# Two gate projections of the second half by seven-product blocks, and another place for the weight-sum jobs

## The chip, the cores and the metric

One core of one Trainium2 chip runs the whole program. The metric is device microseconds of one execution, median of three runs: 1961.64 us (1959.43 to 1966.48) for the kernel before. The engines are TensorE (PE, its weight loads PEld), VectorE (DVE), ScalarE (ACT), GpSimd (POOL) and SyncE (SP), which here only issues transfers. Each engine executes its own queue in order.

## The reference, cut to what matters

One layer: a recurrent branch (RG-LRU), a gated linear attention branch (GLA), each projected to the model width, multiplied by a sigmoid gate and added; then a SwiGLU FFN. The model width is 1024, the FFN 2816, the prompt 1024 tokens, and 8 sequences of 4 sample tokens are beside it.

```python
h = _rmsnorm(x, norm1_g) * (1.0 + sc1) + sh1
u = h @ w_in
u_x, u_g, u_q, u_k, u_v, u_r, u_lr, u_ga, u_gb = jnp.split(u, idx, axis=-1)
xc, new_conv = _causal_conv(u_x, conv_buf, conv_w, conv_b)
h_lru, h_T = _rg_lru(xc, h0, lru_wa, lru_ba, lru_wx, lru_bx, lru_lambda)
y_a = h_lru * jax.nn.gelu(u_g)
...
y_b = o.reshape(B, T, GLA_DV_TOTAL) * jax.nn.silu(u_r)
m = jax.nn.sigmoid(u_ga) * (y_a @ proj_a) + jax.nn.sigmoid(u_gb) * (y_b @ proj_b)
x = (x + gt1 * (m @ w_out)).astype(x.dtype)
h2 = _rmsnorm(x, norm2_g) * (1.0 + sc2) + sh2
f1, f2 = jnp.split(h2 @ ffn_w1, 2, axis=-1)
x = (x + gt2 * ((jax.nn.silu(f1) * f2) @ ffn_w2)).astype(x.dtype)
```

## The kernel before, in words

The tokens are worked in two halves, one after the other: half A (`hf == 0`) has 512 prompt tokens, half B (`hf == 1`) the other 512 and the 32 sample tokens, so 544 columns in two pieces of 272. Features lie on the partitions, in tiles of 128. Every float32 product is made as three matmuls of a rounded high part and a low part of weight and input: `gemm` (L439) issues for each of 8 input tiles and each piece high by high, high by low and low by high. Weights come raw by SP into five `raw` buffers (`load_raw`, L143); `split_w` (L151) makes the high part on ScalarE (L154) and the low part on VectorE (L155) in one of three `hl` buffers, placed by priority some 70 instructions ahead.

`branches` (L1652) runs a half: the attention, with the recurrence `lru` (L1145) as filler; then `y_b_tiles` (L1046), which splits the eight `yb`; then `merge_b`, `merge_a` (or in B `merge_a_fast`), and `back` (output projection, second norm, FFN). `merge_b` (L1182) makes for each of 8 output tiles j the gate product `gbps` (w_in tile T_GB + j, L1189) and the branch product `pbps` (proj_b, L1204), and stores gate times branch in `mb`, a tile of the pool X (8 slots). Half A makes each gate one step ahead. At each yield the rest of the recurrence goes on by two steps: `lru_x` (conv input, `uxps`), `lru_gate` (L1088: `g1`, `g2`, the decay `la` and its partner `hh`), `lru_g` (L1112: `ugps`, the scan, `ya`). The large tiles `ya`, `yb`, `la` and others share the pool S of 17 slots; in half B alone block 9 has its `la` and `lh` in X. T is a pool of six slots.

`merge_a` (half A) makes for each j the gate `gaps` and the branch product `paps` (proj_a, two loads of five tiles, `pa0` and `pa1`). `merge_a_fast` (half B) makes branch products 0 to 3 first and holds them, then couples of two gates by seven products of half the size (`gates_fast`, L1226; `products`, L1410), with sums of input blocks (`block_sums`, L1378) and sums of weight blocks. Couples of the FFN's first product (`ffn1_fast`, L1516; tiles `fa`, `fb`, `fc`, weights `fw`) are made in the same way. Their TensorE order is as written (`as_written`); all else is ordered by a scheduler, by priority and by readiness in a model of time.

The weight sums are made on the fly in half A's and half B's first stages and kept in DRAM. `weight_sums` (L348, `sums_of`): two loads of 512 KB by SP into `raw`, four VectorE operations (L352 to L355), two stores by POOL. `paced_sums` (L362, `sums_late`): 20 jobs of two steps. The first step has for each of two buffers `sums` (there are two in all) a one-column copy on POOL from the tile `pace[0]`, which makes the load wait for that tile, and a load by POOL's queue; the second has four VectorE operations (L392 to L396), the first put behind all VectorE work written before, and two stores by POOL (L398). Jobs 0 to 3 are for FFN couples, 4 to 7 and the last 4 for the second FFN product (384 columns a piece), those between for the gates (256 columns).

```python
            for v in range(2):
                pool.tensor_copy(r[v][:, 0:1], pace[0][:, 0:1])
                pool.dma_start(rv[v], src[v])
            yield 1
```

## Time and profile before

| | us |
|---|---|
| median of the runs | 1961.64 |
| the profiled execution, its own time | 1964.05 |
| its span in the profile | 1962.3 |
| TensorE busy | 1928.1 (98%) |
| VectorE busy | 1361.2 (69%) |
| ScalarE busy | 972.8 (50%) |
| GpSimd busy | 148.8 (8%) |
| mean granted clock | 0.994 |

The profile is of one execution. Busy times are sums over a whole span in which stages have different limits; TensorE's matmuls overlap, so the distance between their starts, not their duration, is what one costs. Along the span half A's merge lies at about 300 to 560 us, its couples 11 to 21 at about 790 to 905, half B's merge at about 1278 to 1533. A wait is named by the instruction that waits and the one that released it.

### The profile page before, as it was taken

Reading aid. Unit: us, or ns where it says so; the run is one execution under the profiler, and the core shown is the slowest. Engines: PE = TensorE matmul, PEld = TensorE weight load, DVE = VectorE, ACT = ScalarE, POOL = GpSimd, SP = SyncE. Lnnn points to the kernel's source line nnn. Section 1 sums busy time; section 2 is a strip of 40 time slices with the busy share of each in tenths; the row PEclk is TensorE's granted clock in tenths of the full one; section 3 lists DMA queues with packets and bytes.
Section 4 is the critical chain, followed back from the end, with each engine's and each line's share of the span. In section 5 each row is a group of like instructions: output and inputs, shape, how many; then the busy total and the mean of one; then the engine's idle time right before and its main releaser. Section 6 shows DMA issues by size and latency. Waiting matters only on the chain. (4 is left out here: it accounts for less than half of the span.)

```text
span 1962.3 us, 33970 instructions
## 1 busy us (share of the span) xinstructions
PE 1928.1 (98%) x13380; PEld 1756.9 (90%) x13380; DVE 1361.2 (69%) x2420; ACT 972.8 (50%) x1559; POOL 148.8 (8%) x279
## 2 busy tenths in 40 slices
PE   9999999998999999999999999999999999999997
PEld 5877777786899998999899998999999999999997
DVE  5648587666658774677674497786467688888867
ACT  4536376533235552555353365665245354666653
POOL 0000001122100000000000001141201000000000
PEclk9999999998999999999999999999999999999999
DMA  8344325476764456554332412334446634555553
GB/s 341 116 154 175 117 92 197 153 262 250 267 227 156 129 179 234 196 185 156 118 119 68 145 50 88 127 121 141 146 140 228 202 130 130 176 169 180 176 164 105
DMA packets 122241, 319.24 MB, mean 163 GB/s; under 512 B 14561, under 2 KB 29665, under 8 KB 122081
## 3 DMA queue, kind: packets, MB, share of 16 engines
q1 hardware_dynamic: 107536, 263.89, 41.5%
q0 software_dynamic: 14000, 52.62, 7.4%
q8 instruction: 105, 1.72, 0.4%
q10 hardware_dynamic: 544, 0.56, 0.1%
q14 instruction: 56, 0.45, 0.1%
HBM read 278.42 MB, written 38.59 MB: 162 GB/s over the span
## 5 line engine op out<-in xcount | busy, mean ns | idle before, releaser
L155 DVE TENSOR_TENSOR fwa_hl<-fwa,fwa_hl 128x1024 fp32r<-128x1024 f32 (+1 forms) x57 | 68.8, 1207 | 44.4 <-ACT fwa_hl L154 43.8
L155 DVE TENSOR_TENSOR fwb_hl<-fwb,fwb_hl 128x1024 fp32r<-128x1024 f32 (+1 forms) x64 | 77.2, 1207 | 27.4 <-ACT fwb_hl L154 27.1
L154 ACT ACTIVATE fwa_hl<-fwa 128x1024 fp32r<-128x1024 f32 (+1 forms) x57 | 59.3, 1040 | 43.7 <-PE fapsa L1431 10.7
L154 ACT ACTIVATE fwb_hl<-fwb 128x1024 fp32r<-128x1024 f32 (+1 forms) x64 | 66.6, 1041 | 23.4 <-PE fcpsb L1431 9.0
L454 PE MATMUL f3psa<-faa,f3a_hl 128*128 128x512 f32 x176 | 68.7, 391 | 1.2 <-DVE f3a_hl L155 1.2
L452 PE MATMUL f3psa<-faa,f3a_hl 128*128 128x512 f32 x176 | 68.7, 390 | 0.6 <-ACT f3a_hl L154 0.6
L453 PE MATMUL f3psa<-faa,f3a_hl 128*128 128x512 f32 x176 | 68.6, 390 | 0.0
L154 ACT ACTIVATE f3a_hl<-f3a_raw 128x768 fp32r<-128x768 f32 (+1 forms) x32 | 25.3, 792 | 56.7 <-PE f3psa L454 37.8
L352 DVE TENSOR_TENSOR s_raw<-s_raw 128x512 f32<-128x512 f32 x16 | 11.1, 692 | 49.3 <-DMA s_raw<-in_ffn 49.3
L454 PEld LDWEIGHTS f3psa<-faa,f3a_hl 128*128 128x128 f32 x176 | 33.0, 188 | 8.9 <-DVE f3a_hl L155 2.1
L452 PEld LDWEIGHTS f3psa<-faa,f3a_hl 128*128 128x128 f32 x176 | 33.0, 188 | 7.7 <-ACT f3a_hl L154 1.0
L453 PEld LDWEIGHTS f3psa<-faa,f3a_hl 128*128 128x128 f32 x176 | 33.1, 188 | 6.8
L155 DVE TENSOR_TENSOR f3a_hl<-f3a_raw,f3a_hl 128x768 fp32r<-128x768 f32 (+1 forms) x32 | 28.3, 888 | 14.3 <-ACT f3a_hl L154 14.3
L454 PE MATMUL wopsb<-mb,wob_hl 128*128 128x272 f32 x128 | 36.9, 288 | 0.0
L452 PE MATMUL wopsb<-mb,wob_hl 128*128 128x272 f32 x128 | 36.9, 289 | 0.0
L453 PE MATMUL wopsb<-mb,wob_hl 128*128 128x272 f32 x128 | 36.8, 288 | 0.0
L453 PE MATMUL wopsa<-ma,woa_hl 128*128 128x256 f32 x128 | 36.4, 284 | 0.0
L454 PE MATMUL wopsa<-ma,woa_hl 128*128 128x256 f32 x128 | 36.2, 283 | 0.0
L452 PE MATMUL wopsa<-ma,woa_hl 128*128 128x256 f32 x128 | 36.1, 283 | 0.0
L1616 POOL DMA_DIRECT2D out_yb<-yb x4 | 2.9, 720 | 407.6 <-DVE yb L1613 406.9
L452 PE MATMUL uxpsa<-h1a,uxpsa_hl 128*128 128x512 f32 x80 | 32.3, 403 | 0.0
L155 DVE TENSOR_TENSOR fvb_hl<-fvb,fvb_hl 128x768 fp32r<-128x768 f32 x28 | 26.8, 956 | 7.7 <-ACT fvb_hl L154 7.3
(2402 smaller groups left out, 7986.7 us busy)
## 6 DMA issues: line engine op xcount, KB each, us to landing
ada<-in_ada_w SPq DMA_DIRECT2D x48, 512.0 KB, 5.5
fwb<-wsum SPq DMA_DIRECT2D x72, 256.0 KB, 3.6
s_raw<-in_ffn SPq DMA_DIRECT2D x32, 512.0 KB, 4.8
wsum<-s_raw POOLq DMA_DIRECT2D x32, 512.0 KB, 3.8
fwa<-wsum SPq DMA_DIRECT2D x64, 256.0 KB, 3.4
fwb<-in_ffn SPq DMA_DIRECT2D x54, 256.0 KB, 3.7
fwa<-in_ffn SPq DMA_DIRECT2D x48, 256.0 KB, 3.2
woa_raw<-in_w_out SPq DMA_DIRECT2D x13, 512.0 KB, 3.6
```

The source lines that it names most:

```text
L154: act.activation(hl[:, 0, :n], raw[:, :n], AF.Copy)
L155: dve.tensor_sub(hl[:, 1, :n], raw[:, :n], hl[:, 0, :n].bitcast(F32))
L352: dve.tensor_add(r2[:, 512:1024], r2[:, 0:512], r2[:, 512:1024])
L452: pe.matmul(out, wh, x[:, o:o + w], start=st, stop=False)
L453: pe.matmul(out, wh, x[:, N + o:N + o + w], start=False, stop=False)
L454: pe.matmul(out, wl, x[:, o:o + w], start=False, stop=en)
L1616: (queues[j // 2 % len(queues)]).dma_start(out[:, j:j + 2, o:o + w], y2)
```

## The change

Half B makes its gates T_GB by couples as well. Its `merge_b` becomes `branch_b`: the eight products with proj_b are made first and copied to `mb`, with three steps of the recurrence at each yield. `merge_fast` makes block sums and four held products (two of them now in `sums` buffers instead of T), then four couples for T_GB (`k`), each followed by the multiplication onto `mb`, and four for T_GA (`h`) as before. The sums of the new couples' weights are eight more jobs, 28 in all. Their places change: in A's `merge_b` at j = 3 to 6 (before 4 to 7), in A's `merge_a` both steps at j = 1 to 5 (before one step at each j), eleven beside A's couples f = 11 to 21 (none before), in half B one at each product of `branch_b` (as many before, beside gate and branch product), none in `merge_fast` (before four). `sums_of` steps in `merge_b` are at j = 0 to 6 (before 1 to 7). In half A too, `la` and `lh` of block 9 are in X. The columns of the w_in tiles from T_GB on are stored in the order KORD.

```diff
--- before.py
+++ after.py
@@ -82,7 +82,7 @@
     axp = ctx.enter_context(tc.tile_pool(name="axp", bufs=2, space=PSUM))
     drp = ctx.enter_context(tc.tile_pool(name="drp", bufs=1, space=bass.MemoryType.DRAM))
     wsum = {f: drp.tile([P, 2048], F32, name=f"wsum{f}") for f in range(FAST[1], NF)}
-    wsumg = [drp.tile([P, 2048], F32, name=f"wsumg{c}") for c in range(GATES)]
+    wsumg = {(t, c): drp.tile([P, 2048], F32, name=f"wsumg{t}_{c}") for t in (T_GB, T_GA) for c in range(GATES)}
     wsum2 = {(q, g): drp.tile([P, 1536], F32, name=f"wsumf{q}{g}") for q in range(4) for g in range(2)}
 
     def S(name, dt=F32):
@@ -377,8 +377,9 @@
         for f in range(FAST[1], FAST[0]):
             columns(wsum[f], [I["ffn1"][2 * f + v] for v in range(2)])
         rows(0)
-        for c in range(GATES):
-            columns(wsumg[c], [I["w_in"][T_GA + 2 * c + v] for v in range(2)])
+        for t in (T_GB, T_GA):
+            for c in range(GATES):
+                columns(wsumg[t, c], [I["w_in"][t + 2 * c + v] for v in range(2)])
         rows(1)
         for k, (u, src, to) in enumerate(jobs):
             r = [wp.tile([P, 768], F32, tag="sums", name=f"sums{k}{v}", bufs=2) for v in range(2)]
...
@@ -1097,7 +1098,7 @@
                 for o, p in s.over(t, g):
                     act.activation(o, p, AF.Tanh, scale=0.5, bias=vh[:, b:b + 1])
             dve.scalar_tensor_tensor(ti[:, :N], ti[:, :N], 1.0, xc[:, :N], op0=OP.add, op1=OP.mult)
-            if s.hf == 0 or nb < NR - 1:
+            if nb < NR - 1:
                 both = S("la" + n)
                 a, hh = both[:, :N], both[:, 544:544 + N]
             else:
@@ -1191,13 +1192,15 @@
                 for t, p in s.over(tg, ps):
                     act.activation(t, p, AF.Tanh, scale=0.5)
 
-            lag = 1 - s.hf
-            if lag:
-                first(0)
+            first(0)
             for j in range(KD):
                 n = f"{s.n}{j}"
-                if j + lag < KD:
-                    first(j + lag)
+                if j + 1 < KD:
+                    first(j + 1)
+                if 3 <= j < 7:
+                    pace[0] = tgs[j]
+                    next(sums_late, None)
+                if j + 1 < KD:
                     yield 5.2
                 tg = tgs.pop(j)
                 p2 = s.wide("pbps" + n)
@@ -1206,12 +1209,27 @@
                 for (t, p), (o, _) in zip(s.over(tg, p2), s.over(m, p2)):
                     dve.scalar_tensor_tensor(o, t, 1.0, p, op0=OP.add, op1=OP.mult)
                 s.mb.append(m)
-                pace[0] = tg
-                if s.hf == 0 and j:
+                if 3 <= j < 7:
+                    next(sums_late, None)
+                if j < 7:
                     next(sums_of, None)
-                if s.hf or j >= 4:
-                    next(sums_late, None)
-                    next(sums_late, None)
+                yield 5.2
+
+        def branch_b(s):
+
+            s.mb = []
+            pace[0] = s.y_b[0][:, :2].bitcast(F32)
+            for j in range(KD):
+                n = f"{s.n}{j}"
+                next(sums_late, None)
+                ps = s.wide("pbps" + n)
+                s.gemm(ps, load_w(I["proj_b"][j], 1024, "pb" + n), 8, s.y_b)
+                m = xp.tile([P, 544], F32, tag="X", name="mb" + n)
+                for o, p in s.over(m, ps):
+                    act.activation(o, p, AF.Copy)
+                s.mb.append(m)
+                pace[0] = m
+                next(sums_late, None)
                 yield 5.2
 
         def gate_a(s, j):
@@ -1223,12 +1241,12 @@
             pace[0] = tg
             return tg
 
-        def gates_fast(s, c, product):
+        def gates_fast(s, b, c, product):
 
             N, W = s.N, s.N // 2
             hi, lo = slice(0, W), slice(W, N)
-            pa, pb, pc = [mm(f"h{k}ps{s.n}{c}")[:, 0, :W] for k in "abc"]
-            v1, v2 = T(f"gc{s.n}{c}"), T(f"gd{s.n}{c}")
+            pa, pb, pc = [mm(f"{b}{k}ps{s.n}{c}")[:, 0, :W] for k in "abc"]
+            v1, v2 = T(f"{b}c{s.n}{c}"), T(f"{b}d{s.n}{c}")
             product(pa, "11", True)
             s.snap(v1[:, lo], pa)
             product(pb, "t1", True)
@@ -1272,34 +1290,40 @@
             s.m = []
             for j in range(KD):
                 tg = s.gate_a(j)
+                if 1 <= j < 6:
+                    next(sums_late, None)
                 s.join(j, tg, s.over(tg, s.branch_a(j)))
                 s.keep_m(j)
-                next(sums_late, None)
+                if 1 <= j < 6:
+                    next(sums_late, None)
                 if j % 3 < 2 and j < 7:
                     next(sums_of, None)
 
-        def merge_a_fast(s):
+        def merge_fast(s):
 
             s.m = []
             N, b, held = s.N, s.block_sums(s.h, "h"), []
             two = S("pa" + s.n)
             for j in range(4):
-                t = two[:, j * N:(j + 1) * N] if j < 2 else T(f"pa{s.n}{j}")[:, :N]
+                next(b, None)
+                t = two[:, j * N:(j + 1) * N] if j < 2 else wp.tile([P, 768], F32, tag="sums", name=f"pa{s.n}{j}", bufs=2)[:, :N]
                 for o, p in s.over(t, s.branch_a(j)):
                     act.activation(o, p, AF.Copy)
                 held.append(t)
-                next(b, None)
             drain(b)
             units = []
-            for c in range(GATES):
-                w1, w2, sm = I["w_in"][T_GA + 2 * c], I["w_in"][T_GA + 2 * c + 1], wsumg[c]
-                units += [w1[:, 0:512], sm[:, 1536:2048], sm[:, 0:512], sm[:, 512:1024], sm[:, 1024:1536], w1[:, 512:1024],
-                          w2[:, 512:1024]]
+            for g in (T_GB, T_GA):
+                for c in range(GATES):
+                    w1, w2, sm = I["w_in"][g + 2 * c], I["w_in"][g + 2 * c + 1], wsumg[g, c]
+                    units += [w1[:, 0:512], sm[:, 1536:2048], sm[:, 0:512], sm[:, 512:1024], sm[:, 1024:1536], w1[:, 512:1024],
+                              w2[:, 512:1024]]
             begin = len(traced())
             product = s.products(units, 512, s.bs, "gw" + s.n)
             for c in range(GATES):
-                tgs = s.gates_fast(c, product)
-                next(sums_late, None)
+                for m, t in zip(s.mb[2 * c:], s.gates_fast("k", c, product)):
+                    dve.scalar_tensor_tensor(m[:, :N], t[:, :N], 1.0, m[:, :N], op0=OP.add, op1=OP.mult)
+            for c in range(GATES):
+                tgs = s.gates_fast("h", c, product)
                 if c == GATES - 1:
                     s.keep_m(*range(2 * c))
                 for i in range(2):
@@ -1307,8 +1331,6 @@
                     s.join(j, tg, [(tg[:, :N], held[j])] if j < 4 else s.over(tg, s.branch_a(j)))
                     if c == GATES - 1:
                         s.keep_m(j)
-                    if j >= 4:
-                        next(sums_late, None)
             drain(sums_late)
             as_written(begin, (mybir.EngineType.PE,))
 
@@ -1536,6 +1558,8 @@
                 product(pa, "t2", False)
                 s.snap(v1[:, hi], pa)
                 product(pb, "22", False)
+                if s.hf == 0 and f >= 11:
+                    next(sums_late, None)
                 yield 6
                 product(pa, "t3", False)
                 s.snap(v2[:, hi], pa)
@@ -1552,6 +1576,10 @@
                     s.late = tg
                 else:
                     s.keep(f, tg)
+                if s.hf == 0:
+                    if f >= 11:
+                        next(sums_late, None)
+                    pace[0] = tg
                 yield 4.5
             as_written(begin, (mybir.EngineType.PE,))
 
@@ -1667,15 +1695,17 @@
             mix(chain(iter([6]), s.head_norm(1)), fill)
             drain(r)
             s.y_b_tiles()
-            for w in s.merge_b():
+            for w in s.branch_b() if s.hf else s.merge_b():
                 next(l, None)
                 next(l, None)
+                if s.hf:
+                    next(l, None)
                 s.ada(1)
             drain(l)
             drain(s.adas)
             if s.hf:
                 pool.dma_start(O["tails"], tails)
-            s.merge_a_fast() if s.hf else s.merge_a()
+            s.merge_fast() if s.hf else s.merge_a()
             s.back()
 
     A, B = Half(0), Half(1)
...
```

## Rows read from the trace of the kernel before

**Rows 1.** The page, part 1: busy us (share of the span) and instructions

```profile
PE 1928.1 (98%) x13380; PEld 1756.9 (90%) x13380; DVE 1361.2 (69%) x2420; ACT 972.8 (50%) x1559; POOL 148.8 (8%) x279
```

**Rows 2.** TensorE's waits, whole span: us in total, times, longest

```profile
PE papsa L454 <- DVE pa1a_hl L155: 7.5, 1, 7.5
...
PE hbpsb L1429 <- ACT t12hb L1403: 0.9, 1, 0.9
```

**Rows 3.** Stretches: us, PE PEld DVE ACT POOL busy (instructions), clock, DMA share, GB/s

```profile
460.00:480.00 20.00, 12.52 (x43) 9.58 (x42) 14.85 (x25) 7.56 (x10) 10.48 (x10) 0.74 0.57 199
...
480.00:500.00 20.00, 20.00 (x90) 16.57 (x89) 11.94 (x17) 5.95 (x8) 2.42 (x5) 1.00 0.79 274
...
785.00:905.00 120.00, 120.00 (x967) 118.38 (x966) 83.96 (x120) 67.38 (x108) 2.13 (x4) 1.00 0.60 194
...
1380.00:1400.00 20.00, 20.00 (x163) 20.00 (x162) 8.34 (x16) 4.30 (x7) 4.67 (x8) 1.00 0.47 159
```

**Rows 4.** Order of time, VectorE: start, us, line, out<-in, count [idle before]

```profile
453.10 0.69 DVE L352 TENSOR_TENSOR s_raw<-s_raw 128x512 f32<-128x512 f32 x1 [5.74 <-DMA s_raw<-in_ffn]
...
463.75 0.43 DVE L392 TENSOR_TENSOR sums<-sums 128x256 f32<-128x256 f32 x1 [3.95 <-DMA sums<-in_ffn]
...
468.87 0.82 DVE L155 TENSOR_TENSOR pa1a_hl<-pa1a_raw,pa1a_hl 128x640 fp32r<-128x640 f32 x1
```

**Rows 5.** Order of time, ScalarE, block 9 of half A

```profile
416.10 0.68 ACT L1098 ACTIVATE tia<-g2a,vh 128x512 f32<-128x512 f32 x1
...
448.12 0.80 ACT L1106 ACTIVATE laa<-tra,sp 128x512 f32<-128x512 f32 x1
```

**Rows 6.** Order of time, TensorE: two products, two block products

```profile
1381.80 0.29 PE L452 MATMUL gbpsb4l<-h1b,gbpsb_hl 128*128 128x272 f32 x1
...
1387.77 0.29 PE L452 MATMUL pbpsb4l<-ybb,pbb_hl 128*128 128x272 f32 x1
...
1476.24 0.29 PE L1429 MATMUL hbpsb<-h1b,gwb_hl 128*128 128x272 f32 x1
...
1477.75 0.29 PE L1429 MATMUL hapsb<-t3hb,gwb_hl 128*128 128x272 f32 x1
```

**Rows 7.** Order of time, TensorE, couples of half A's FFN

```profile
839.83 0.28 PE L1429 MATMUL fcpsa<-h2a,fwa_hl 128*128 128x256 f32 x1
...
847.02 0.28 PE L1429 MATMUL fbpsa<-h2a,fwa_hl 128*128 128x256 f32 x1
...
849.89 0.28 PE L1429 MATMUL fcpsa<-h2a,fwa_hl 128*128 128x256 f32 x1
```

**Rows 8.** Order of time, VectorE and GpSimd, a job of half B

```profile
1394.86 0.42 DVE L392 TENSOR_TENSOR sums<-sums 128x256 f32<-128x256 f32 x1 [0.48 <-DMA sums<-in_w_in]
...
1397.98 0.73 POOL L398 DMA_DIRECT2D wsumg<-sums  x1 [0.93 <-DVE sums L396]
...
1400.94 0.19 POOL L387 COPY sums<-gbb 128x1 f32<-128x1 f32 x1 [0.75 <-DMA wsumg<-sums]
1401.18 1.43 POOL L388 DMA_DIRECT2D sums<-in_w_in  x2
```

**Rows 9.** Transfers in 1275:1435, then 300:460: KB each, median us to landing

```profile
sums<-in_w_in POOLq DMA_DIRECT2D x16, 256.0 KB, 3.3
...
sums<-in_ffn POOLq DMA_DIRECT2D x8, 256.0 KB, 4.9
...
wsum<-sums POOLq DMA_DIRECT2D x6, 256.0 KB, 5.6
```

**Rows 10.** Order of time, VectorE, a split in half A's FFN couples

```profile
842.60 1.23 DVE L155 TENSOR_TENSOR fwa_hl<-fwa,fwa_hl 128x1024 fp32r<-128x1024 f32 x1 [0.72 <-ACT fwa_hl L154]
```

**Rows 11.** Order of time, TensorE and VectorE, start of half B's merge

```profile
1277.56 0.29 PE L452 MATMUL gbpsb0l<-h1b,gbpsb_hl 128*128 128x272 f32 x1
...
1288.97 5.17 DVE L189 TENSOR_TENSOR ybb<-srb,ybb 128x544 fp32r<-128x544 f32 x8
```

**Rows 12.** Instructions on the tile sums: duration ns min/median/max, starts

```profile
L387 POOL COPY sums<-gbb x16: 179/185/1076, 1285.1 to 1424.1; 128x1 f32<-128x1 f32 x16
```

More of the change, by code (lines that the diff above doesn't have):

```diff
@@ L665, in proj_h @@
             ps = s.wide(name)
-            s.gemm(ps, w_in_tile(t, name), KD, s.h, split=split, order=KORD if T_GA <= t < T_GB else None)
+            s.gemm(ps, w_in_tile(t, name), KD, s.h, split=split, order=KORD if t >= T_GA else None)
             return ps
@@ L1753, in _pack @@
     wi = _tiles(np.concatenate([w[:, :o[6]], w[:, o[7]:]], 1))
-    wg = wi[T_GA:T_GB].reshape(T_GB - T_GA, P, KD, P)[:, :, list(KORD)]
-    wi[T_GA:T_GB] = wg.reshape(T_GB - T_GA, P, D)
+    wg = wi[T_GA:].reshape(len(wi) - T_GA, P, KD, P)[:, :, list(KORD)]
+    wi[T_GA:] = wg.reshape(len(wi) - T_GA, P, D)
     a["w_in"] = wi
```

## The prediction

> **What bounds the kernel now.** Begin with the shares of the engines on the page: TensorE is busy 1928.1 us, 98% of the span [rows 1]. Nothing but TensorE work, or one of its few stalls, can shorten this kernel, and any other engine matters only where it makes TensorE wait. So the second view is the list of TensorE's waits. One is large: `papsa` in line 454 waits 7.5 us, once, for VectorE's split of `pa1a_hl` [rows 2]. The third view, the stretches, shows what that stall costs in all: 460 to 480 us issued 43 matmuls of 512 columns where the next 20 us issued 90, and its granted clock averaged 0.74, so part of it at the lower of the two levels, 1.2 and 2.4 GHz, where the next stretch has 1.00 [rows 3]. 47 matmuls at 20/90 = 0.222 us are 10.4 us: 7.5 of waiting and about 2.9 in which the matmuls after it ran at the low level. The fourth view, the order of time on VectorE and ScalarE, says why. VectorE executes its queue in order, and stood 5.74 us for a load of `s_raw` (a sum job of `weight_sums`) and 3.95 us for the load of a paced sum job (L392), both queued ahead of the split that TensorE needed [rows 4]. ScalarE had the last recurrent block's gate input at 416.10, but its decay `laa` came at 448.12 [rows 5]: that tile takes a slot of the pool S (17 slots), which then holds eight `ya`, eight `yb` and one older `la`; the slot came free when the last product with `yb` began. The recurrence's tail (L1122 to L189) then ran in front of the split too.
>
> **The change, part by part.** Sums are made against the profiled execution, 1964.05 us (span 1962.3 and 1.75 around it), which is 2.4 above the median of the three runs, 1961.64; the forecast is moved down by that 2.4.
>
> (a) *First half, its last block and its jobs.* `la9` and `lh9` now come from pool X also in half A. X has 8 slots; the branch products hold at most six until block 9 ends, so the wait for S goes and the chain of block 9 starts some 30 us earlier. Jobs run at j = 3..6 in place of 4..7, none at the last product nor at the first `merge_a` step, and the `sums_of` jobs are one step earlier (0..6). Nothing on VectorE then waits for a transfer just before `pa1a_hl`. Gain: 10.4 us at most, 0 at least; I take all, because both causes in [rows 4, 5] are removed.
>
> (b) *Second half, first gates by blocks.* Removed: 8 products of 48 matmuls; one lasts 1387.77 - 1381.80 = 5.97 us, 47.8 us together. Added: 4 couples of 7 block products; one is 1477.75 - 1476.24 = 1.51 us, a couple 10.57, four 42.3 [rows 6]. Gain 5.5 us. Weight splits grow from 2048 to 3584 columns a couple on ScalarE and VectorE; the existing gate couples carry this load without a stall, so it costs nothing there.
>
> (c) *Block sums* of h start one product earlier, and two of the held products lie in the `sums` slots, not in T (six slots, of which the block sums take four at a time). The stall of `hbpsb` at the first couple, 0.9 us [rows 2], should go: gain 0.9, at least 0.
>
> (d) *Jobs beside A's couples 11 to 21.* The 8 new jobs, and those moved, make 11 jobs here, one in each couple. A couple lasts 849.89 - 839.83 = 10.06 us [rows 7]. VectorE is busy 84.0 of 120 us [rows 3], 7.0 a couple; four additions at 0.42 [rows 8] make 8.7: it fits. What may not fit is the job's own loop, since both `sums` buffers belong to one job: additions, stores by POOL, landing, pacing copies, loads, landing. From one job of half B [rows 8]: first addition 1394.86 to second store 1397.98 is 3.1 us; the next copy, released by that store's landing, is at 1400.94, 3.0 later; the two loads begin at 1401.18 and take 1.43, so the second begins 1.0 after the copy; it lands 3.3 later (the median in that stretch [rows 9]). Loop: 10.4 us. With the landings of the first half's stretch, 5.6 for the store and 4.9 for the load [rows 9], it is 14.6. The DMA share of the couples is 0.60 [rows 3], already above the 0.47 of half B's stretch, before the jobs add 1 MB a couple (256 KB four times), but they have no bursts of 512 KB loads, as that first stretch has; so I stay near the lower end: load 3.9, store 3.0, loop 11.0. When the loop is longer than the couple, L392 blocks VectorE, with the splits behind it and TensorE behind those. Cover: a split ends at 843.83 and its first matmul is at 847.02, 3.2 us [rows 7, 10]. Ten intervals of 0.94 less 3.2: **cost 6 us**; ends 0 (10.4 gives 3.4 of lag, all but covered) and 42 (14.6).
>
> Beside this stands a price that only a page gives: the Trainium skill, DMA: Bandwidth & Descriptors, section on the anatomy of one DMA on the GpSimd path, fits such a transfer with 2.0 us plus bytes over 436 GB/s, an estimate of 2.6 us for 256 KB. By it the loop is 9.3 us, below the couple, and (d) costs nothing; the landings of [rows 9], 3.3 to 5.6, are all longer, so the trace doesn't bear it out here.
>
> (e) *`merge_a` of A:* five jobs in steps 1 to 5, one a step, where before one took two steps. A step is 24 + 30 matmuls, 12.0 us at 0.222. With the landings of that half the loop is 14.6, so lag grows by 2.6 in four intervals, 10.4; one split tile of 15 matmuls covers 3.3. Ends 0 and 7; I take 3.5.
>
> (f) *Start of `branch_b`:* its first product needs all `yb`, where the removed gate product stood between. That one began at 1277.56, and the eight splits of `yb` lasted from 1288.97 to 1294.14, 0.65 us each [rows 11]. In place of the gate product `ux7` and `ug5`, which followed it, can run from 1277.56, at 5.97 each until 1289.5; by then the first `yb` is there, and the others come faster than the product eats them (0.75 us a tile). I take 0; if the product is queued ahead of `ug5`, 6.
>
> (g) *End of `branch_b`:* products 5 to 7 have no recurrent work between, 5.97 us each, with a job of 10.4 each: VectorE waits some 4 and then 9 us. What queues behind L392 are the splits for `proj_a` and the block sums; two split tiles are ahead. I take 2; ends 0 and 6.
>
> Other edits (names, order of w_in columns, the pace variable) cost nothing: matmul count and bytes are the same. The jobs that left `merge_fast` hid no wait, so that is nothing either.
>
> Sum: -10.4 - 5.5 - 0.9 + 6 + 3.5 + 0 + 2 = -5.3; 1964.05 - 5.3 - 2.4 = **1956 us**.
>
> **The rivals.**
> *R1, the loops keep pace.* (d), (e) and (g) cost 0 to 6 together, because landings are near 3 us: -16.8 to -10.8, so 1945 to 1951. For it: in half B at a cadence of 11.9 us L392 waited only 0.48 us [rows 8]. Against: the couples are shorter and the DMA share higher.
> *R2, slower: the pacing copies are late.* In each job POOL's two copies stand between landing and load. They take 0.18 us as a rule and 1.08 at the worst [rows 12]; on a VectorE busy nine tenths both may be near the worst, 1.8 us more, so the loop is 12.8, and (d) costs 10 times 2.7 less 3.2, 24 us. With (e) at 7 and (g) at 6 the sum is +20: 1982. It decides against the change as soon as the loop of (d) is above 11.5 us, where it costs 11.3 and (e) and (g) at 5.5 eat the rest. The rule behind such lateness is in the Trainium skill, SBUF — State Buffer, section Who interferes with whom: a VectorE instruction with two SBUF inputs keeps out a GpSimd instruction that reads SBUF until it ends; of the 16 copies in [rows 12] the median is at the minimum, so the trace bears it out for few.
> *R3, the change doesn't do what it says in A:* the stall at `papsa` stays or moves by a step, since jobs are denser there: -6.4 + 11.5 = +5, 1967.
>
> **How the numbers follow.** Forecast (costs of 6 to 20 together) 0.42, R1 0.33, R2 0.16, R3 0.09. A measurement of this kernel can tell about 0.5%, 9.8 us, from no change. Faster by more (below 1951.8): R1 and a little of the forecast, 0.36. Slower by more (above 1971.4): R2 and a little of R3, 0.17. Within: 0.47. Range: 1944 (all gains, no cost) to 1975 (R2 with half of its price beyond the forecast).
>
> **What would show it.** (a) No wait of `papsa` above 2 us near 470, clock 1.00, and `laa` of block 9 within 5 us of its tanh. (b) 336 matmuls of the k-couples where 384 of `gbpsb` were. (c) No wait of `hbpsb`. (d) The distance of `fcpsa` between couples: 10.06 if the loop keeps pace, 11 if it binds, with `sums` L392 waiting for DMA each time. (e), (g) L392's waits in 490 to 560 and near the last `pbpsb`. The prediction is wrong if A's couples keep 10.06 us (faster), or if they take above 12 (slower).

## The result, and the profile after

The change makes the kernel slower. The kernel after takes 2025.62 us (2022.01 to 2032.46), the kernel before 1964.02 in the same runs, a ratio of 1.0322 (95% interval 1.0307 to 1.0338); the forecast was 1956 us with a range up to 1975. The page of after, its span, the engines and the first addition of the paced jobs (L393, L392 before):

```profile
span 2026.2 us, 34080 instructions
PE 1940.8 (96%) x13332; PEld 1763.9 (87%) x13332; DVE 1381.1 (68%) x2462; ACT 990.2 (49%) x1593; POOL 185.0 (9%) x327
...
L393 DVE TENSOR_TENSOR sums<-sums 128x256 f32<-128x256 f32 (+1 forms) x28 | 12.9, 461 | 89.2 <-DMA sums<-in_w_in 68.5
```

TensorE has 12.7 us more busy time than in [rows 1] for 48 matmuls fewer, so a part ran at the lower level of its clock, and idles some 51 us more. The last row is the lead: the 28 first additions found VectorE idle for 89.2 us, waiting for the jobs' loads; the 20 of the kernel before waited 4.5 us. TensorE's waits, in half A's merges, in couples 11 to 21 with the start of half B, and from half B's u_x products on (us in total, times, longest):

```profile
PE gapsa L455 <- DVE gapsa_hl L155: 6.4, 4, 4.1
...
PE fapsa L1453 <- DVE fwa_hl L155: 7.8, 4, 2.2
PE nps1b L460 <- DVE acc1b L488: 7.7, 1, 7.7
PE fapsa L1451 <- ACT vaa L1459: 4.2, 7, 0.9
PE fbpsa L1453 <- DVE fwa_hl L155: 4.1, 3, 3.0
...
PE pbpsb0l L453 <- ACT ybb L188: 7.4, 1, 7.4
PE papsb1l L455 <- DVE pa0b_hl L155: 6.5, 1, 6.5
PE pbpsb1l L453 <- ACT trb L1099: 6.5, 1, 6.5
PE pbpsb3l L453 <- ACT trb L1099: 2.0, 1, 2.0
```

[rows 2] show two waits, `papsa` 7.5 and `hbpsb` 0.9. Both are gone, and these nine, with others of 2.3 us and less, stand in their place. The stretches (us, then busy time of PE, PEld, DVE, ACT and POOL, PE clock, DMA share, GB/s):

```profile
790.00:902.00 112.00, 97.73 (x767) 95.03 (x766) 71.45 (x119) 53.28 (x84) 27.36 (x42) 0.97 0.68 212
902.00:955.00 53.00, 38.95 (x239) 33.77 (x238) 32.91 (x56) 21.63 (x36) 14.29 (x24) 0.94 0.64 202
1280.00:1360.00 80.00, 63.62 (x433) 59.34 (x432) 55.51 (x111) 42.05 (x74) 18.30 (x28) 0.85 0.35 111
1444.00:1484.00 40.00, 33.19 (x243) 32.53 (x242) 23.86 (x43) 13.53 (x27) 6.41 (x8) 0.87 0.51 158
1484.00:1526.00 42.00, 42.00 (x338) 42.00 (x337) 25.80 (x32) 24.29 (x42) 0.00 (x0) 1.00 0.56 173
```

[rows 3] had 785 to 905 without a gap at clock 1.00. Only the last of these five, the k couples, is like that now. The first start of a tile's matmuls in each trace (for the couples the last start of `fapsa`) gives the account by stretch; before and after are differences of two such starts, the last column is the growth:

| stretch | before | after | change |
|---|---|---|---|
| start to half A's output product (`wopsa` 562.0, 559.4) | 562.0 | 559.4 | -2.6 |
| from there to the end of the couples (last `fapsa` 902.9, 926.2) | 340.9 | 366.8 | +25.9 |
| to half B's norm and u_x products (`uxpsb0l` 1155.4, 1192.3) | 252.5 | 266.1 | +13.6 |
| to the first held product (`papsb0l` 1429.6, 1443.6), 47.8 us of gate products gone | 274.2 | 251.3 | +24.9 beside those 47.8 |
| four held products (to 1459.5, 1483.5) | 29.9 | 39.9 | +10.0 |
| k couples (to 1525.6) | 0 | 42.1 | 5.7 less than the 47.8 |
| h couples and the rest (`wopsb` 1533.1, 1597.5) | 73.6 | 71.9 | -1.7 |

Together +64.4; the spans differ by 63.9. The k couples bring what (b) said; the loss is elsewhere, where the jobs stand. The first additions beside the couples, in order of time on VectorE, with what each waited:

```profile
819.08 0.42 DVE L393 TENSOR_TENSOR sums<-sums 128x256 f32<-128x256 f32 x1 [2.68 <-DMA sums<-in_w_in]
831.86 0.42 DVE L393 TENSOR_TENSOR sums<-sums 128x256 f32<-128x256 f32 x1 [4.95 <-DMA sums<-in_w_in]
845.20 0.43 DVE L393 TENSOR_TENSOR sums<-sums 128x256 f32<-128x256 f32 x1 [4.11 <-DMA sums<-in_w_in]
858.31 0.42 DVE L393 TENSOR_TENSOR sums<-sums 128x256 f32<-128x256 f32 x1 [5.16 <-DMA sums<-in_w_in]
874.05 0.42 DVE L393 TENSOR_TENSOR sums<-sums 128x256 f32<-128x256 f32 x1 [6.53 <-DMA sums<-in_w_in]
...
938.30 0.42 DVE L393 TENSOR_TENSOR sums<-sums 128x256 f32<-128x256 f32 x1 [5.18 <-DMA sums<-in_w_in]
```

From 804.82 to 938.30 eleven additions follow each other at 13.35 us on average, where a couple has 10.06 [rows 7]. One round, on POOL:

```profile
833.04 0.71 POOL L399 DMA_DIRECT2D wsumg<-sums  x1 [4.97 <-DVE sums L395]
834.97 0.73 POOL L399 DMA_DIRECT2D wsumg<-sums  x1 [1.22 <-DVE sums L397]
835.70 0.82 POOL L388 COPY sums<-fta 128x1 f32<-128x1 f32 x1
836.82 0.71 POOL L389 DMA_DIRECT2D sums<-in_w_in  x1 [0.30 <-POOL sums L388]
839.22 0.18 POOL L388 COPY sums<-fta 128x1 f32<-128x1 f32 x1 [1.69 <-DMA wsumg<-sums]
839.70 0.73 POOL L389 DMA_DIRECT2D sums<-in_w_in  x1 [0.30 <-POOL sums L388]
```

From the first addition (831.86) to the second store (834.97) 3.1 us as in [rows 8]; to the copy that this store's landing released (839.22) 4.25, not 3.0; to the next first addition (845.20), which the load issued at 839.70 released, 6.0. That is the loop named in (d); POOL is busy for 3.9 us of it and waits for the rest.

### The profile page after: what moved, and what is told of

Read it like the earlier page. It is cut to its first block, busy times and chain, and to the rows that moved or that the text cites. A ratio compares the mean times of both kernels' runs of the same rounds, so it can differ in the third digit from the quotient of the medians.

```text
span 2026.2 us, 34080 instructions
## 1 busy us (share of the span) xinstructions
PE 1940.8 (96%) x13332; PEld 1763.9 (87%) x13332; DVE 1381.1 (68%) x2462; ACT 990.2 (49%) x1593; POOL 185.0 (9%) x327
## 5 line engine op out<-in xcount | busy, mean ns | idle before, releaser
L393 DVE TENSOR_TENSOR sums<-sums 128x256 f32<-128x256 f32 (+1 forms) x28 | 12.9, 461 | 89.2 <-DMA sums<-in_w_in 68.5
L455 PE MATMUL f3psa<-faa,f3a_hl 128*128 128x512 f32 x176 | 69.7, 397 | 3.5 <-DVE f3a_hl L155 3.4
L155 DVE TENSOR_TENSOR gwb_hl<-gwb,gwb_hl 128x1024 fp32r<-128x1024 f32 x28 | 34.3, 1225 | 27.1 <-ACT gwb_hl L154 23.4
L352 DVE TENSOR_TENSOR s_raw<-s_raw 128x512 f32<-128x512 f32 x16 | 11.1, 691 | 46.4 <-DMA s_raw<-in_ffn 46.4
```

The costliest lines, as they stand in the source:

```text
L155: dve.tensor_sub(hl[:, 1, :n], raw[:, :n], hl[:, 0, :n].bitcast(F32))
L352: dve.tensor_add(r2[:, 512:1024], r2[:, 0:512], r2[:, 512:1024])
L393: dve.tensor_add(r2[:, 1], r2[:, 0], r2[:, 1])
L455: pe.matmul(out, wl, x[:, o:o + w], start=False, stop=en)
```

## The experiments

Theory L: the jobs' loop through their two buffers is longer than the work beside it, and since the addition stands in VectorE's queue ahead of splits, the whole kernel goes at the loop's pace. Rivals: D1, the jobs' traffic makes weights late; D2, VectorE has too much arithmetic; and for half B, Q (the order of TensorE's queue) and V (VectorE is late there without any job). Where gate couples read sums of other weights instead of a job left out, size and traffic stay. A time without a range is that of one execution; the kernel before took from 1957.4 to 1967.2 us in its own, so small differences are read from the stretches of the traces, not from the totals.

**Couples without jobs (e1).**

```diff
-                if s.hf == 0 and f >= 11:
-                    next(sums_late, None)
...
-                    if f >= 11:
-                        next(sums_late, None)
...
+            if 9 <= k < 20:
+                continue
```

> The eleven sum jobs beside couples 11 to 21 of half A are left out (additions, loads, copies and stores); the gate couples that would read their sums read other sums of the same size, so the output differs. The kernel after takes 2025.6 us; there couples 11 to 21 end 25.9 us late against before and half B's norm another 13.7. Theory L (loop): the jobs' own round through their two buffers takes 13.4 us where a couple has 10.06 us of matmuls, and its first addition, standing in VectorE's queue, stops the couple's splits; the jobs' copies and stores on POOL's queue also delay half B's load of x. L expects the last couple product near 903 us (926 with the jobs), half B's norm product near 920 (953), and 1986 us in all (1982 to 1992). Theory D (traffic or VectorE's load, not the loop) expects the same here, and is told apart by the next runs. Theory E (the couples are late for what stands ahead of them, la9 and lh9 or the denser jobs of the merges) expects the couples to stay over 915 and the time over 2010.

Measured: 1980.8 us, before 1957.4 beside it. From half A's output product to the last couple product 339.6 us (after 366.8, before 340.9), from there to the norm product of half B 16.0 (27.0, 16.1). Between 790 and 930 TensorE has no wait. So the jobs cost the couples 27 us and half B's start 11; theory E is out. The time is 1 us below the expected 1982 to 1992, and still 23.4 over before: the rest lies in half B, whose stretch from the first u_x product to `wopsb` is 20.0 us longer than before.

**No additions (e2).**

```diff
-            dve.tensor_add(r2[:, 1], r2[:, 0], r2[:, 1])
+            if not 9 <= k < 20:
+                dve.tensor_add(r2[:, 1], r2[:, 0], r2[:, 1])
+                ...
```

> Beside couples 11 to 21 of half A the jobs keep their copies, loads and stores, and only their four additions on VectorE are left out (the sums stored there are the raw halves, so the output differs). Theory L (a VectorE that stands at the jobs' additions): the couples run at 10 us again, the last product near 903 to 906 us; half B's x load still stands behind copies and stores on POOL's queue, so part of the 13.7 us at half B's start stays: 1988 to 2002 us. Theory D1 (the traffic of the jobs makes the couples' weights late): the couples stay some 20 us late and the time over 2015. Theory D2 (VectorE's arithmetic): like L.

Measured: 2000.35 us. The couples take 342.9, 3.3 over e1: not 27. With all transfers and no additions, the stretch 820 to 902 was full, at a higher DMA share than in the kernel after:

```profile
820.00:902.00 82.00, 82.00 (x678) 81.59 (x677) 59.84 (x89) 47.71 (x78) 27.16 (x44) 1.00 0.83 262
PE f3psa L454 <- ACT f3a_hl L154: 6.2, 1, 6.2
PE nps1b L461 <- DVE acc1b L489: 4.9, 1, 4.9
...
912.24 2.16 POOL L543 DMA_DIRECT2D xb<-in_xb  x4
917.38 0.66 ACT L487 ACTIVATE sq1b<-xb 128x544 f32<-128x544 f32 x1 [12.69 <-DMA xb<-in_xb]
```

The same stretch of after has PE busy 67.7 us, a DMA share of 0.67 and 212 GB/s. So 262 GB/s don't hold TensorE up, and D1 falls. Half B's start stays late (28.6 us): its four loads of x stand behind the jobs on POOL, where the first came at 896.98 before, at 912.24 here and at 935.74 in the kernel after; ScalarE stood 12.69 us at the first square of x, with the splits for `f3psa` behind it.

**Additions alone (e2b)**, always on the pair of tiles that job 9 loaded:

```diff
+            if not 10 <= k < 20:
+                r = [wp.tile(...)]
+                ...
-            for v in range(2):
+            for v in range(2 if not 9 <= k < 20 else 0):
                 pool.dma_start(to[v], rv[v])
```

> Beside couples 11 to 21 of half A the four additions of each job stand where they stood, 1.7 us of VectorE in every couple, but always on the same tiles, which were loaded once; loads, copies and stores of these jobs are left out (the couples that would read the sums read others, so the output differs). Theory L: nothing to wait for, so the couples cost nearly what they cost without jobs: 1986 to 1994 us, last couple product before 910. Theory D1 (traffic): the same. Theory D2 (VectorE's arithmetic is what is too much): couples near 920 to 926 and 2005 to 2012 us.

Measured: 1979.07 us, 7 below the range that L expected; couples 342.3: D2 falls. Against e1, additions without transfers cost 2.7 us in eleven couples and transfers without additions 3.3; both, with the wait between them, 27.2.

**Half the rate (e3).**

```diff
-                    if f >= 11:
+                    if f == 11:
                         next(sums_late, None)
...
+            if 9 <= k < 15:
+                continue
```

> Jobs beside couples 11 to 21 at half the rate: one step of a job in a couple, not two (both in the first); the six jobs 9 to 14 are left out and their gate couples read other sums of the same size, so the output differs. A job's round now has two couples, 20 us. Theory L: 13.4 is less than 20, VectorE doesn't wait for loads, the couples run at 10 to 10.3 us and the last product is near 903 to 907 us; half B's start still has one job's stores ahead of its x load: 1988 to 1996 us. Theory D1 (traffic, or D2, arithmetic): half the jobs leave half the loss, the last product near 914 and 2003 to 2010 us.

Measured: 1995.36 us, within L's range; couples 348.5, start of half B 16.0. But the last couple product is at 911.6, between L's 903 to 907 and the 914 of half a loss: half the jobs left a third of the loss, not half and not nothing. The trace tells which:

```profile
PE fapsa L1453 <- ACT vaa L1461: 4.7, 1, 4.7
...
822.19 0.43 DVE L395 TENSOR_TENSOR sums<-sums 128x256 f32<-128x256 f32 x1 [5.39 <-DMA sums<-in_w_in]
841.45 0.42 DVE L395 TENSOR_TENSOR sums<-sums 128x256 f32<-128x256 f32 x1
861.57 0.42 DVE L395 TENSOR_TENSOR sums<-sums 128x256 f32<-128x256 f32 x1
881.69 0.42 DVE L395 TENSOR_TENSOR sums<-sums 128x256 f32<-128x256 f32 x1
901.81 0.42 DVE L395 TENSOR_TENSOR sums<-sums 128x256 f32<-128x256 f32 x1
```

(L395 is the first addition.) The job with both its steps in the first couple left too little time for the next load, 5.39 us of waiting; the four after it stand 20.12 us apart, two couples of 10.06, and wait for nothing. Nearly all the loss is that one wait, 4.7 us of TensorE and the clock after it (0.96 from 820 to 902).

**Half B: the queue's order (e4b), the jobs (e5b), and both (e45)**, on top of e1.

```diff
+            for _ in range(3 * s.hf):
+                next(l, None)
             for w in s.branch_b() if s.hf else s.merge_b():
```

```diff
-            if 9 <= k < 20:
+            if 9 <= k < 28:
                 continue
```

> The kernel of the run e1_couples_without_jobs (23.4 us over the kernel before on its chip), in which three more steps of the recurrence (the products ux7 and ug5 and what goes with them) are issued ahead of half B's second-branch products. In e1 the first of these, pbpsb0, stands in TensorE's order ahead of ux7 and waits 7.7 us for the last block of y_b. Theory Q (the order of the queue): ux7 and ug5 have 12 us of matmuls and cover it; the wait goes with the clock lost behind it, 8 to 11 us: 12 to 16 us over the kernel before. Theory V (VectorE is late in this stretch whatever the order): a wait of like size comes up at ux7, ug5 or the next product, and the time stays 20 to 24 us over before. The output differs as in e1.

> The kernel of the run e1_couples_without_jobs, in which the eight jobs beside half B's second-branch products are left out as well (their readers read other sums of the same size). In e1 TensorE waits 6.3 us at pbpsb1 and 4.7 us at papsb1, where VectorE stands 5.6 to 6.2 us at a job's first addition. Theory L: both waits go with the clock lost behind them, 11 to 16 us: 7 to 12 us over the kernel before; the 7.7 us at pbpsb0 stay. Theory V (VectorE's other work in this stretch is too much once the gate products beside it are gone): the waits stay for the most part, and the time is 17 to 23 us over before.

> Both edits of e4b_x_products_first and e5b_branch_b_without_jobs. Theories Q and L: TensorE has no wait of over 1 us from ux0 to the last couple, and what is left against the kernel before is the prediction's own sum without the jobs: -2.6 us to the end of half A's merges, 0 in the couples, -5.5 us for the couples in place of products and -0.9 us for the block sums: 6 to 12 us under before. Theory V: not under the time before.

Measured: 1973.71, 1963.65 and 1962.71 us, before 1961.53 beside them: 12.2, 2.1 and 1.2 over it. The first lies at the edge of Q's range; the second is 5 below L's 7 to 12. By the starts of the first u_x product and of `wopsb`, which leave half A out, the stretch takes 397.7 in e1, 393.3, 382.6 and 377.4; 377.7 before. TensorE's waits there, in e1, in the one without jobs and in both:

```profile
PE pbpsb0l L455 <- ACT ybb L188: 7.7, 1, 7.7
PE pbpsb1l L455 <- ACT trb L1101: 6.3, 1, 6.3
PE papsb1l L457 <- DVE pa0b_hl L155: 4.7, 1, 4.7
```

```profile
PE pbpsb0l L455 <- ACT ybb L188: 7.7, 1, 7.7
PE pbpsb3l L455 <- ACT trb L1101: 0.5, 1, 0.5
PE pbpsb1l L455 <- ACT trb L1101: 0.5, 1, 0.5
```

```profile
PE pbpsb0l L455 <- ACT trb L1101: 3.9, 1, 3.9
```

Without jobs the waits at `pbpsb1` and `papsb1` go, 15.1 us with the clock behind them: theory L holds here too, and V falls. In e1 VectorE stood 6.23 us at the addition of 1303.96 and 5.58 at that of 1399.45, just ahead of those two. With the order alone (e4b) `pbpsb0` waits 3.6 us, `pbpsb1` no longer, but 6.9 us come up at `papsb2` for the split of `pa0b_hl`. The order Q brings 4.4 and 5.2, not 8 to 11: `pbpsb0` no longer waits for `ybb`, but for ScalarE's `trb`, which must read the PSUM tile that it wants (3.9 us), so the expectation of no wait over 1 us failed. With both the time was not under before, against the 6 to 12 expected. From the first u_x product to the first held product e45 takes 233.6 us, 7.2 more than before less its 47.8 of gate products: this wait and the clock behind it take what the couples give. (Up to the first u_x product the three differ from each other by 6 us, so the stretch is the measure, not the time.)

**Part (a) alone (e6)**, on the kernel before.

```diff
-            if s.hf == 0 or nb < NR - 1:
+            if nb < NR - 1:
...
-                if s.hf == 0 and j:
+                if s.hf == 0 and j < 7:
...
-                if s.hf or j >= 4:
+                if s.hf or 3 <= j < 7:
```

> The kernel before with one part of the change alone: la9 and lh9 of half A lie in the pool of the 8 wide tiles, as in half B, and the jobs of half A's second-branch merge come one product earlier; the output is the same. The prediction's first term is 10.4 us for this (the 7.5 us at the first first-branch product, and the clock behind it). The kernel after showed -2.6 us there, but with denser jobs beside the gates, which cost it 6.4 us at a gate's weights. Theory P (the term holds by itself, the denser jobs ate it): 8 to 11 us faster, a ratio of 0.9945 to 0.996. Rival (the stall only moves to the jobs' additions): 0 to 4 us, a ratio over 0.998.

Measured: 1952.3 us (1948.79 to 1954.12), 0.9953 of before (0.9937 to 0.9970): half a per cent faster, with an interval clear of 1, as theory P has it. Its largest wait of TensorE from 440 to 610 us is this:

```profile
PE f1psa L452 <- ACT h2a L531: 0.6, 1, 0.6
```

The output product starts at 550.4, 11.6 earlier than before. In the kernel after it was 2.6, so 9 us were lost to something else in half A.

**The first merge as before (e10)**, in the kernel after: both job steps and the weight sum behind each product.

```diff
-                if 3 <= j < 7:
-                    pace[0] = tgs[j]
-                    next(sums_late, None)
...
+                pace[0] = tg
+                if j < 7:
+                    next(sums_of, None)
                 if 3 <= j < 7:
                     next(sums_late, None)
-                if j < 7:
-                    next(sums_of, None)
+                    next(sums_late, None)
```

> The kernel after, in which half A's first-branch merge takes its job steps and weight sums as the kernel before does (both steps and the weight sum behind each product, one product earlier), while the denser jobs of the second merge, the couples and all of half B stay as they are; the output is the same. The kernel after reaches the output product of half A at 559.4 us, e6_state_in_the_other_pool at 550.4, and e8_whole_change_slow_jobs, which has the split steps of the kernel after and the sparse jobs of the kernel before in the second merge, at 556.7. Theory S (the split steps shift the weight sums so that one addition stands ahead of the second gate's weights): 550 to 553 us there, and 2017 to 2021 us in all. Theory M (the denser jobs of the second merge): 558 to 560 us, and 2022 to 2028 us.

Measured: 2021.46 us, output product at 553.9, between the two theories. By these traces the split steps account for 5.5 of the 9 us, the denser jobs of the second merge for the 3.5 left. The sizes are rough: the kernel after and the eight others here that share both merges with it reach the output product between 556.6 and 563.1. How the steps do it shows in VectorE's order. First e6, then after (s_raw is a weight sum's tile, `gapsa_hl` the second gate's weights):

```profile
460.89 0.69 DVE L352 TENSOR_TENSOR s_raw<-s_raw 128x512 f32<-128x512 f32 x1 [6.57 <-DMA s_raw<-in_ffn]
462.95 1.22 DVE L155 TENSOR_TENSOR gapsa_hl<-gapsa_raw,gapsa_hl 128x1024 fp32r<-128x1024 f32 x1
```

```profile
467.95 0.69 DVE L352 TENSOR_TENSOR s_raw<-s_raw 128x512 f32<-128x512 f32 x1 [7.14 <-DMA s_raw<-in_ffn]
470.01 1.22 DVE L155 TENSOR_TENSOR gapsa_hl<-gapsa_raw,gapsa_hl 128x1024 fp32r<-128x1024 f32 x1
```

In both a weight sum stands ahead of that split and waits for its load, 6.57 and 7.14 us; with the split steps it comes 7 us later, and so does the split. The direction is firm: in the ten traces with split steps this split starts at 467.5 to 471.1, in the three without them (e6, e9, e10) at 463.0 to 463.6.

**The last two couples free (e11).**

```diff
-                if s.hf == 0 and f >= 11:
+                if s.hf == 0 and 11 <= f < 20:
...
+            if 9 <= k < 11:
+                continue
```

> The kernel after without jobs beside the last two couples of half A (jobs 9 and 10 are left out and their gate couples read other sums of the same size, so the output differs). Theory O (POOL's order: half B's x load stands behind the last job's copies and stores): from the last couple's product to half B's norm product 16 us as before (27.0 in the kernel after), and with two couples at 10 us the total falls by 13 to 18 us, to 2007 to 2013 us. Theory D1 (x comes late through traffic): the 27 us stay within 3, and the total is 2018 us or more.

Measured: 2009.45 us; 16.0 us from the last couple product to the norm product. Theory O: the x loads were late by POOL's order. The couples themselves got only 0.8 us shorter (366.0), which I had not expected: the last couple product comes 13.1 us behind the ninth addition in both kernels (911.53 and 924.6 here, 913.12 and 926.2 in the kernel after), so nine rounds, not eleven, set that end.

**The whole change with slow jobs, twice (e8, e9).** All 28 jobs, one step in each of couples 6 to 21 and of the k and h couples, eight in half B's branch products, the held products 2 and 3 in T, two steps of the recurrence ahead of `pbpsb0`.

```diff
-                if s.hf == 0 and f >= 11:
-                    next(sums_late, None)
...
-                    if f >= 11:
-                        next(sums_late, None)
+                    next(sums_late, None)
...
+            for _ in range(2 * s.hf):
+                next(l, None)
```

The first version has the remaining eight steps beside half A's first second-layer part. The second has them beside the held products and the last four products with `proj_a`, and half A's first merge as in e10.

> The whole change (four k couples in place of eight gate products, la9 and lh9 in the other pool, all 28 sum jobs, the reference's output), with the jobs spread so that a job's round always has some 15 to 25 us: one step in each product of half A's first-branch merge as before, one in each of the 8 products of A's first second-layer part and in each of its couples 6 to 21, eight in half B's second-branch products, one in each k and h couple; the held products 2 and 3 lie in tiles of the small pool as before, and two steps of the recurrence go ahead of pbpsb0. Theory L: none of the additions waits over 2 us, the couples run at 10 to 10.3 us, half B's x load is not late, and the time is that of e6_state_in_the_other_pool less the change's own 5 to 7 us plus what stays at pbpsb0 (up to 4 us): 1944 to 1954 us, a ratio to before of 0.991 to 0.997. Rival (more jobs cost by their number, through traffic and VectorE's arithmetic, some 0.5 us for each of the eight added and as much for those that lost their old cover): 1955 to 1970 us.

> The whole change with its 28 jobs (the reference's output), spread anew after e8_whole_change_slow_jobs: half A's first-branch merge takes its steps as the kernel before, nothing beside the second-layer part (8 steps of e8 there, where TensorE waited 4.8 us for weights), one step in each of couples 6 to 21, eight beside half B's second-branch products, one beside each held product, one in each k and h couple and one beside each of the four last first-branch products. Theory L: e8's losses in half A's merges (6.3 us) and second-layer part (some 4 us) go: 1953 to 1959 us, and e6_state_in_the_other_pool, the first part alone at 1952.3, stays the fastest or equal, because eight more jobs cost about what the four couples save. Rival (the change still has its full 5 to 7 us once no job waits): 1943 to 1949 us. Rival (the steps beside the held products wait and stop VectorE): over 1960 us.

Measured: 1967.48 us, 1.0031 of before (1.0018 to 1.0043), and 1951.08 us (1950.32 to 1951.29), 0.9945 (0.9927 to 0.9963). The first missed L's range and lies in its rival's. Its additions waited only 11.4 us in all, but one, at the end of the second-layer part, stood 6.06 us ahead of weight splits; VectorE also stood 8.60 us for the load of a `weight_sums` job (L352, at 773.64), ahead of the split of `f3a_hl` for which TensorE then waited 3.0; and the split steps of the first merge were still there. Against the rival (each job costs, by its number) speaks the second, 16 us shorter with as many jobs. It has the lowest median of the study, between the 1943 to 1949 of its own rival and the expected 1953, but it isn't told apart from e6, so the 5.7 us of the k couples show in the traces and in no total:

```profile
span 1949.5 us, 34086 instructions
PE 1921.5 (99%) x13332; PEld 1750.4 (90%) x13332; DVE 1380.2 (71%) x2462; ACT 989.2 (51%) x1593; POOL 182.8 (9%) x327
...
L393 DVE TENSOR_TENSOR sums<-sums 128x256 f32<-128x256 f32 (+1 forms) x28 | 12.8, 457 | 10.5 <-DMA sums<-in_w_in 10.5
```

The same 28 jobs with the same bytes as in the kernel after wait 10.5 us in place of 89.2, and TensorE is busy 99% of the span.

## Why the prediction was wrong

The steps that failed most are (f) and (g), which took the start of `branch_b` as free and its jobs as nearly so, and (d), whose loop was given landings too short; one term was left out. Against the terms of the sum, half A's merges came out 4.3 us worse ((a) and (e): 6.9 less predicted, 2.6 measured), the couples 19.9 (d), the start and end of `branch_b` 32.9 ((f) and (g): 2 predicted, 24.9 and 10.0 measured), and 13.6 us at half B's start stand in no term; (b) and (c) came out 1.0 better. That is the 69.7 us between -5.3 and +64.4.

(a) Right in mechanism and size: 10.4 predicted, 11.6 in e6. In the whole change it brought 2.6, together with (e). R3 is what came there, at another product: the step that failed is "nothing on VectorE then waits for a transfer just before `pa1a_hl`": true of that split, not of the second gate's.

(b), (c) Right: 5.5 predicted, 5.7 measured in every trace with k couples; the wait of `hbpsb` is gone.

(d) The form was right (the loop against the couple, L392 blocking VectorE) and a term of it was mis-sized. I took 11.0 us, "near the lower end", from landings of half B's calm stretch; 13.35 was measured, toward the 14.6 of the busy end. In the couples' stretch the DMA rows were:

```profile
wsumg<-sums POOLq DMA_DIRECT2D x16, 256.0 KB, 3.7
sums<-in_w_in POOLq DMA_DIRECT2D x16, 256.0 KB, 5.0
```

5.0 and 3.7 us where I had 3.9 and 3.0. I had noted that the couples' DMA share is above half B's, and then chose the quieter rows; the difference to the couple is multiplied by ten. With 13.35 the same sum gives 10 times 3.29 less 3.2, 29.7; measured were 25.9, since the last two rounds no longer held the couples (e11). By the estimate that I quoted from the Trainium skill, DMA: Bandwidth & Descriptors, section on the anatomy of one DMA on the GpSimd path, 2.6 us, the loop would have been 9.3; here the landings are 1.4 and 1.9 times that. The cost was 25.9 where I had 6. R2's place and its direction were right, but that its 24 for a loop of 12.8 comes close is in part luck, since the copies were the small part of it: in [rows 12] their median was at the minimum, and beside the couples it was this (ns min, median, max; below it the split beside the copy of 835.70):

```profile
L388 POOL COPY sums<-fta x19: 179/423/1028, 809.1 to 929.6; 128x1 f32<-128x1 f32 x19
...
835.25 1.22 DVE L155 TENSOR_TENSOR fwa_hl<-fwa,fwa_hl 128x1024 fp32r<-128x1024 f32 x1
```

A quarter of a microsecond more at the median. By the rule of the Trainium skill, SBUF — State Buffer, section Who interferes with whom, they are held up by VectorE's two-input instructions. This trace bears it out for eleven of the 19: they took 0.34 us or more, and each ended 0.03 to 0.05 us after such an instruction did, as the copy of 835.70 (to 836.52) after the split of 835.25 (to 836.47).

Left out of the sum altogether: POOL's queue behind the last job. Half B's x loads stand in it, ScalarE's squares of x and the splits behind them wait, and 13.6 us were lost to the u_x products. The step that moves jobs past a queue's other work has to list that work.

(e) 3.5 predicted with half A's loop; the denser jobs cost about that, 3.5 by e10 against e6, and the split steps of the first merge, which I had counted as part of the gain, 5.5; both sizes are rough, as said there.

(f) I took 0 and named 6 for the case that the product is queued ahead of `ug5`. It was queued ahead of `ux7` as well, and waited 7.4 us. e45 shows that my picture for 0 was wrong too: with both ahead, the PSUM tile is the next wait (3.9).

(g) 2 predicted for the end of `branch_b`, from two jobs there; the jobs blocked VectorE from its first product on. All eight first additions of half B waited, 1.35 to 7.29 us, where before one did, for 0.48; the second stood ahead of a split for u_x (`uxpsb_hl`):

```profile
1347.70 0.43 DVE L393 TENSOR_TENSOR sums<-sums 128x256 f32<-128x256 f32 x1 [7.29 <-DMA sums<-in_w_in]
```

TensorE's waits were 6.5, 2.0 and 6.5 us; in e1 such waits cost some 15 us with the clock after them (e5b against e1). The landings weren't longer than before: 3.1 us for a load and 2.6 for a store of 256 KB from 1275 to 1435, [rows 9] have 3.3 for the load. I had priced the jobs in half B as before because their number is the same, but the removal of the gate products took the time that covered their loop.

So the kernel got slower as R2 said, at three times R2's price, because (d), (f), (g) and the x loads failed in one direction: in all four, work that TensorE needs stands in an in-order queue behind something late. In (d) that is a transfer whose time I took from a quieter stretch, in (g) a loop of ordinary length (11.3 us from 1336.36 to 1347.70) with too little work left beside it, in (f) the order of TensorE's own queue, and the x loads' place in POOL's queue I left out.

What stays open: the start and end of `branch_b` lost 34.9 us in the kernel after and 27.5 in e1, with the same eight jobs there. And in e9 the stretch from half B's u_x products to the held ones takes 4.2 us more than before less its gate products, with no new wait over 1.0 us. Part of that is the clock: from 1245.7 to 1255.7 it is 0.72, with 41 matmuls where the kernel before has 62 at 1.00 in the same place (1255.4 to 1265.4), by estimate 2.5 us at 0.12 a matmul; why it fell isn't shown.

## What to carry to other kernels

A background job that passes through buffers has a round of its own; its operation on a busy in-order engine belongs where the round, priced with landings of the busiest stretch it runs through, is surely over. Here eleven such jobs cost the couples 25.9 us at one per couple of 10 us; eight at one per two couples cost them nothing that shows (e9: 340.3 us from the output product to the last couple product, before 340.9). When work is removed from a stretch, price again what it covered; and when a job moves onto a queue, list every transfer that now stands behind it.

## What the runs showed of the hardware

Landings were longer in the busier stretches: a load of 256 KB took 3.3 us in half B's stretch [rows 9], at a DMA share of 0.43, and 5.0 beside the couples, at 0.67. The share alone doesn't give them: from 815 to 925 they took 4.0 in e3, 5.3 in e9 and 5.1 in e2, at 0.72, 0.65 and 0.79. And that load was no limit for TensorE: at 0.83 and 262 GB/s (e2) the couples ran without a gap. In stretches with waits of 4 to 8 us the granted clock was lower: 0.87 over the 40 us of the held products, which lost 6.5 us to the wait and 3.5 more, 0.85 over the 80 us of `branch_b`'s start; it was 1.00 in the k couples behind them, which have no wait.
